# An encoder step whose input projection goes from plain column blocks, interleaved with the other work, to Strassen pairs done first

## The chip, the cores and the metric

The kernel runs on one core of a Trainium2 chip. The metric is the time of one execution in device microseconds (us). Names of the engines in the profile: PE is the matrix engine and PEld its weight loads, DVE the vector engine, ACT the scalar engine, POOL the GpSimd engine, SP the engine that issues the DMAs.

## The reference

One layer of a streaming encoder for 1088 tokens: 1024 of a new stream and 64 that continue another one. D is 1024, all in fp32.

```python
def hybrid_layer(x, p, st, past_k, past_v):
    h = rms_norm(x, p['norm_pre'])
    proj = h @ p['w_in']
    lru_x, lru_g, ssd_z, ssd_xbc, ssd_dt, cf_in, cf_g, sb_qkv, sb_g, merge = split_cols(proj, IN_SPLITS)
    lru_xc, lru_conv_new = causal_dwconv(lru_x, st['lru_conv'], p['lru_conv_w'], p['lru_conv_b'])    # 4 taps
    lru_h, lru_h_new = rg_lru(lru_xc, ...);  u_a = lru_h * jax.nn.silu(lru_g)
    xbc, ssd_conv_new = causal_dwconv(ssd_xbc, ...)                                                  # 4 taps
    y, ssd_new = ssd_scan(...);  u_b = rms_norm((y + D * xh) * jax.nn.silu(ssd_z), p['ssd_norm'])
    glu = cf_in[..., :CF_W] * jax.nn.sigmoid(cf_in[..., CF_W:])
    cfc, cf_conv_new = causal_dwconv(glu, ...)                                                       # 31 taps
    u_c = jax.nn.silu(layer_norm(cfc, ...)) * jax.nn.silu(cf_g)
    o = stick_breaking(q, k, v);  u_d = o * jax.nn.silu(sb_g)
    y_br = jnp.einsum('btnc,ncd->btnd', jnp.stack([u_a, u_b, u_c, u_d], axis=2), p['w_down'])
    mixed = jnp.sum(jax.nn.sigmoid(merge.reshape(bsz, t, N_BRANCH, D_MODEL)) * y_br, axis=2)
    return x + rms_norm(mixed @ p['w_out'], p['norm_post']), new
```

The input projection `h @ w_in` has 80 blocks of 128 columns and 8 columns more (`ssd_dt`). 32 of the 80 blocks are the gates of the four merges (`merge`).

## The kernel before

A product in fp32 is made of three matmuls on a high and a low part of each operand: `mm3` (L104 to L107) issues high by high, low by high and high by low. A column block of the projection takes 8 steps over D for each of three pieces of the tokens (256, 384 and 448 columns, `SPL`), so 72 matmuls. Its weights come by one DMA of 512 KB (`weights`, L90), ACT makes the high part (L97) and DVE the low one (L98).

The order of PE's instructions is written by hand: a generator (`Work`, `Feed`, L120 to L170) hands out one piece of a projection or of a merge at each `feed.step()`, and the chains of the other branches call it between their own steps. So the chains (on ACT, DVE and POOL) run while PE works on the projection. The other engines' orders come from the scheduler, by data dependences and by priorities (`ATT_PRIO`, `CONV_PRIO`, `W_PRIO`). Results of the projection go to the consumer from PSUM; a few (SiLU paths, `spill`) wait in DRAM. In order of time:

- the head (to 45 us): RMSNorm, transposes, the high and low part of h (`hh`, `hl`), beside the first two V blocks
- 45 to 580 us: the attention with 68 units (one of 8 heads by one of 8 query blocks of 128, and 4 units of the 64 tokens), fed with K, Q, V, gate, convolution-module and SiLU blocks. A unit is: score matmuls to PSUM `pz` (one buffer); two sigmoids on ACT (L430, L431); the causal mask on two 128x128 corners by POOL's affine_select (L435); a scan over the keys (L438) and a product (L439) on DVE; transposes on PE (L450), a copy on ACT (L452), the output matmuls (L468). The 31-tap convolution of the conv module runs on DVE at low priority (L239)
- 580 to 742 us: RG-LRU, with its projections, and the SSD's inputs (short convolutions, L239)
- 742 to 875 us: LayerNorm of the conv module, beside the first merge
- 875 to 1240 us: the SSD's scan in 9 chunks, beside merges 0 to 2. A merge takes a gate block (projection, sigmoid on ACT L689), the product with w_down (`down`, 12 matmuls for each piece), and DVE multiplies and adds (L698, L699)
- 1240 to 1336 us: the 8 gate blocks of the last merge, projections alone
- from 1336 us: the last merge's products with w_down, then w_out with the final RMSNorm

Of the kernel before, what the change touches and what calls it, by code (L numbers as in the profile page):

```python
# [16 lines left out]
D = 1024  # L17
EPS = 1e-6
SPL = ((0, 256), (256, 384), (640, 448))
NM = 448  # L20
# [4 lines left out]
OFF = 128 * 1088  # L25

LNA, LNB = (2, 2, 2), 5
ATT_PRIO, CONV_PRIO, W_PRIO, H_PRIO = 3000, 600, 300, 1000
# [17 lines left out]
def encoder_step(ctx, tc, x, prm, win, wdt, wdn, wout, lwa, lwx, ckT, cv_, ssd0, npre, npost, dtb, alog, dskip,  # L46
# [6 lines left out]
    hp = ctx.enter_context(tc.tile_pool(name="hT", bufs=1))  # L53
    wp = ctx.enter_context(tc.tile_pool(name="wts", bufs=2))
    ps = ctx.enter_context(tc.tile_pool(name="ps", bufs=1, space=PSUM))
    dr = ctx.enter_context(tc.tile_pool(name="scr", bufs=1, space=DRAM))
    uh_d = [dr.tile([128, 4, T], FT, name=f"uh{b}") for b in range(4)]
    ul_d = [dr.tile([128, 4, T], FT, name=f"ul{b}") for b in range(4)]
    xbc_d = dr.tile([128, 8, T], FT, name="xbc")
    sz_d = dr.tile([128, 4, T], FT, name="sz")  # L60
    lg_d = dr.tile([128, 4, T], FT, name="lg")
    cg_d = dr.tile([128, 4, T], FT, name="cg")
    cv_d = dr.tile([128, 4, T], FT, name="cv")

# [37 lines left out]
    hl = [hp.tile([128, 8, n], FR, name=f"hl{i}") for i, (_, n) in enumerate(SPL)]

# [4 lines left out]

    def rstd(st, r, n, w=1):
# [10 lines left out]
    class Work:  # L120
        """A chain of matrix work: its first stretch fetches operands, each later one is a piece of the tokens."""

        def __init__(self, gen):
            self.gen, self.ready, self.room = gen, False, False

        def prime(self):
            if not self.ready:
                self.ready = True
                next(self.gen)
            return self  # L130

        def step(self):
            self.prime()
            r = next(self.gen, self)
            self.room = r is True
            return r is not self

        def drain(self):
            while self.step():
                pass  # L140

    class Feed:
        """Matrix work issued between the steps of another chain."""

        def __init__(self):
            self.queue, self.later = [], []

        def add(self, *gens):
            self.queue.extend(Work(g) for g in gens)

        def defer(self, n, fn):
            self.later.append([n, fn])

        def step(self, n=1):
            for _ in range(n):
                while self.queue and not self.queue[0].step():
                    self.queue.pop(0)
                if len(self.queue) > 1 and self.queue[0].room:
                    self.queue[1].prime()
                for e in self.later:  # L160
                    e[0] -= 1
                for e in [e for e in self.later if e[0] <= 0]:
                    self.later.remove(e)
                    e[1]()

        def drain(self):
            while self.queue or self.later:
                self.step()

    feed = Feed()  # L170

    def project(p, n, i, hi, lo):
        for k in range(8):
            mm3(p[:, :n], hi[:, k, :], lo[:, k, :], hh[i][:, k, :], hl[i][:, k, :], k == 0, k == 7)

    def proj(chunk, evac, pt=pj, done=None):
        hi, lo = weights(win[chunk])
        yield
        for i, (t0, n) in enumerate(SPL):
            p = pt()  # L180
            project(p, n, i, hi, lo)
            evac(t0, n, p)
            if i == 2 and done is not None:
                done()
            yield True


    ctx.enter_context(tc.manual_schedule(engines={mybir.EngineType.PE}))
    warm = const.tile([128, 1], FT, name="warm")
    S.activation(warm, eps_t, AF.Sqrt)  # L190

    def head(hd, g_bc, tiles):
        w = len(tiles)
        st = hd.tile([128, 4 * w], FT, name="st", bufs=4)
        xs = []
        for e, i in enumerate(tiles):
            r = 128 if i < 8 else 64
            xt = hd.tile([128, D], FT, name="xt", bufs=9)
            dma(xt[:r], x[i * 128:i * 128 + r, :])
            if i == 0:  # L200
                dma(g_bc, ap(npre, 0, [[0, 128], [1, D]]))
            if r < 128:
                V.memset(st[r:, e:e + 1], 1.0)
            sq = hd.tile([128, D], FT, name="sq", bufs=1)
            S.activation(sq[:r], xt[:r], AF.Square, accum_out=st[:r, e:e + 1])
            xs.append(xt)
        rstd(st, 128, D, w)
        for e, i in enumerate(tiles):
            r = 128 if i < 8 else 64
            hn = hd.tile([128, D], FT, name="hn", bufs=4)  # L210
            V.scalar_tensor_tensor(hn[:r], xs[e][:r], st[:r, w + e:w + e + 1], g_bc[:r], op0=OP.mult, op1=OP.mult)
            j, o = WHERE[i]
            nk = 8 if i % 2 else 4
            for q in range(0, 8, nk):
                p = pz() if nk == 8 else pg()
                p3 = p.rearrange("p (k c) -> p k c", c=128)
                for k in range(nk):
                    PE.transpose(p3[:, k, :r], hn[:r, (q + k) * 128:(q + k + 1) * 128], ident[:r, :r])
                ks, dst = slice(q, q + nk), slice(o, o + r)
# [852 lines left out]
```

## Time and profile before

| | |
|---|---|
| time, median of 3 runs | 1494.03 us (1493.73 to 1494.9) |
| span of the profiled execution | 1490.9 us |
| median less that span | 3.1 us |
| PE busy | 1460.1 us (98%), 9157 matmuls |
| DVE busy | 921.1 us (62%) |
| ACT busy | 588.5 us (39%) |
| POOL busy | 118.9 us (8%) |
| MATMUL lines of the projection (L105 to L107 with `hh`, `hl`) | 637.6 + 631.8 + 631.5 us, 5760 matmuls |

The page gives the span of the profiled execution, without a time of its own; the 3.1 us between that span and the median of the runs stand in for what lies around it. A matmul's duration (some 330 ns) is its own length; since matmuls are pipelined, the next one starts earlier, and cost is read from the distance between starts. DVE and ACT instructions run one after another, so their durations add up, with a small overlap. The three projection lines above overlap in the same way and hold some 960 us of PE's time.

### The profile page before, as it was taken

The numbers are of one execution on the slowest core, as the hardware profiler recorded it, in microseconds if no ns is written. First come the engines' busy times: TensorE is split into PE (matmuls) and PEld (weight loads), VectorE is DVE, ScalarE is ACT, GpSimd is POOL, SyncE is SP. The second block draws the span as 40 slices with busy tenths as digits, with TensorE's granted clock in tenths as the row PEclk, the third lists the DMA queues.
The fourth block names the chain that finished last, engine by engine and source line by source line (L and its number), as shares of the span: only waits on it lengthen the run. The fifth ranks groups of instructions, "written<-read, shape, count | busy, mean of one in ns | idle before, by whom it ended". The sixth has DMA issues, their size and how long they took to land.

```text
span 1490.9 us, 23008 instructions
## 1 busy us (share of the span) xinstructions
PE 1460.1 (98%) x9157; PEld 1360.5 (91%) x9157; DVE 921.1 (62%) x1379; ACT 588.5 (39%) x1000; POOL 118.9 (8%) x157
## 2 busy tenths in 40 slices
PE   6999999999999999999999999999999999999997
PEld 5898999999999998999999999999999999999885
DVE  6289589579769955677765554656655541019433
ACT  6323434443453344666644322333332332124211
POOL 0003212231221222000000000000000000000000
PEclk9999999999999999999999999999999999999999
DMA  6232212313212323454433354222621234113322
GB/s 209 75 87 63 72 61 68 103 44 89 92 46 87 98 87 109 138 117 107 116 124 116 110 169 142 82 68 83 196 78 57 75 88 148 51 43 113 99 85 71
DMA packets 103339, 144.17 MB, mean 97 GB/s; under 512 B 20800, under 2 KB 82112, under 8 KB 103232
## 3 DMA queue, kind: packets, MB, share of 16 engines
q1 hardware_dynamic: 103232, 142.71, 31.9%
q8 instruction: 72, 1.18, 0.3%
q14 instruction: 35, 0.29, 0.1%
HBM read 97.95 MB, written 40.53 MB: 93 GB/s over the span
## 4 chain that ended last, share of the span: by engine, by line
PE 87%; issue 6%; DVE 4%; DMA 1%; ACT 1%; POOL 1%; SPq 0%; DVEq 0%; POOLq 0%; ACTq 0%
PE pj L105 24%; PE pj L106 24%; PE pj L107 24%; PE pg L468 2%; PE pg L450 2%; PE pg L106 1%; PE pg L107 1%; PE pg L105 1%; DVE cvo L239 1%; PE pz L417 1%; PE pz L418 1%; PE pg L878 1%; PE pg L736 1%; PE pg L871 1%; DMA g_bc<-in_npre_dram 0%
## 5 line engine op out<-in xcount | busy, mean ns | idle before, releaser
L105 PE MATMUL pj<-hh,w_hi 128*128 128x384 f32 (+2 forms) x1920 | 637.6, 332 | 1.7 <-ACT hh L220 1.7
L106 PE MATMUL pj<-hl,w_hi 128*128 128x384 f32 (+2 forms) x1920 | 631.8, 329 | 1.8 <-DVE hl L221 1.8
L107 PE MATMUL pj<-hh,w_lo 128*128 128x384 f32 (+2 forms) x1920 | 631.5, 329 | 0.0
L105 PEld LDWEIGHTS pj<-hh,w_hi 128*128 128x128 f32 x1920 | 363.6, 189 | 16.6 <-issue 2.1
L106 PEld LDWEIGHTS pj<-hl,w_hi 128*128 128x128 f32 x1920 | 363.7, 189 | 14.4 <-DVE hl L221 2.6
L107 PEld LDWEIGHTS pj<-hh,w_lo 128*128 128x128 f32 x1920 | 363.5, 189 | 11.0
L98 DVE TENSOR_TENSOR w_lo<-w_raw,w_hi 128x1024 fp32r<-128x1024 f32 x96 | 117.5, 1224 | 226.9 <-ACT w_hi L97 226.7
L97 ACT ACTIVATE w_hi<-w_raw 128x1024 fp32r<-128x1024 f32 x96 | 101.7, 1060 | 281.7 <-PE pj L106 262.6
L239 DVE SCALAR_TENSOR_TENSOR cvo<-cbuf,p_t,cvo 128x1118 f32<-128x1118 f32 x120 | 165.6, 1380 | 2.1
L105 PE MATMUL pj<-uh,w_hi 128*128 128x384 f32 (+2 forms) x384 | 126.2, 329 | 0.0
L107 PE MATMUL pj<-uh,w_lo 128*128 128x384 f32 (+2 forms) x384 | 126.2, 329 | 0.0
L106 PE MATMUL pj<-ul,w_hi 128*128 128x384 f32 (+2 forms) x384 | 126.1, 328 | 0.0
L438 DVE TENSOR_TENSOR_SCAN fb<-fb,ones 128x128 f32<-128x128 f32 (+8 forms) x68 | 90.0, 1324 | 38.0 <-POOL fb L435 37.4
L435 POOL TENSOR_SCALAR_AFFINE_SELECT beta<-beta 128x128 f32<-128x128 f32 (+1 forms) x72 | 78.2, 1086 | 14.4 <-ACT beta L431 13.7
L698 DVE TENSOR_TENSOR sg<-pj,sg 128x256 f32<-128x256 f32 (+2 forms) x48 | 25.7, 535 | 84.9 <-PE pj L107 80.6
L689 ACT ACTIVATE sg<-pj 128x256 f32<-128x256 f32 (+2 forms) x72 | 33.7, 468 | 112.2 <-PE pj L107 112.0
L105 PEld LDWEIGHTS pj<-uh,w_hi 128*128 128x128 f32 x384 | 72.7, 189 | 2.3
L106 PEld LDWEIGHTS pj<-ul,w_hi 128*128 128x128 f32 x384 | 72.6, 189 | 2.2
L107 PEld LDWEIGHTS pj<-uh,w_lo 128*128 128x128 f32 x384 | 72.6, 189 | 2.2
L435 POOL TENSOR_SCALAR_AFFINE_SELECT fb<-fb 128x128 f32<-128x128 f32 (+1 forms) x72 | 38.2, 530 | 449.2 <-ACT fb L430 354.4
L439 DVE TENSOR_TENSOR beta<-beta,fb 128x128 f32<-128x128 f32 (+8 forms) x68 | 50.3, 740 | 4.3 <-POOL beta L435 0.7
L452 ACT ACTIVATE wT<-pg 128x512 f32<-128x512 f32 (+3 forms) x96 | 43.3, 485 | 18.1 <-PE pg L450 17.8
(313 smaller groups left out, 1683.0 us busy)
## 6 DMA issues: line engine op xcount, KB each, us to landing
w_raw<-in_win_dram SPq DMA_DIRECT2D x80, 512.0 KB, 3.7
w_raw<-in_wdn_dram SPq DMA_DIRECT2D x16, 512.0 KB, 3.6
xt<-in_x_dram SPq DMA_DIRECT2D x8, 512.0 KB, 10.5
xbc<-xs SPq DMA_DIRECT2D x8, 512.0 KB, 2.6
xb<-xbc SPq DMA_DIRECT2D x8, 512.0 KB, 4.9
w_raw<-in_wout_dram SPq DMA_DIRECT2D x8, 512.0 KB, 3.7
xr<-in_x_dram SPq DMA_DIRECT2D x8, 512.0 KB, 3.8
out_y_dram<-yo SPq DMA_DIRECT2D x16, 256.0 KB, 2.3
```

Of the source, the lines that this page charges most:

```text
L97: S.activation(hi, r3, AF.Copy)
L98: V.tensor_sub(lo, r3, hi.bitcast(FT))
L105: PE.matmul(out, ah, bh, start=first, stop=False)
L106: PE.matmul(out, ah, bl, start=False, stop=False)
L107: PE.matmul(out, al, bh, start=False, stop=last)
L239: V.scalar_tensor_tensor(out[:, :n], b[:, i:i + n], w[:, i:i + 1], out[:, :n], op0=OP.mult, op1=OP.add)
L435: G.affine_select(t_[s, 1024 - w:1024], t_[s, 1024 - w:1024], pattern=[[-1, w]], compare_op=OP.is_gt, fill=fill, base=0, channel_multiplier=1)
L438: V.tensor_tensor_scan(F[:, rev], F[:, rev], ones[:, 0:1].to_broadcast([128, n]), 1.0, OP.mult, OP.mult)
L439: V.tensor_tensor(B[:, L:1024], B[:, L:1024], F[:, L + 1:1025], op=OP.mult)
L450: PE.transpose(p[:, (j - j0) * 128:(j - j0 + 1) * 128], B[:, L + j * 128:L + (j + 1) * 128], ident)
L452: S.activation(wT[:, j0:j1, :], p[:, :(j1 - j0) * 128].rearrange("p (j c) -> p j c", c=128), AF.Copy)
L689: S.activation(sg[:, :n], p[:, :n], AF.Sigmoid)
```

## The change

The 1088 tokens are cut into halves of 544 and each half into quarters of 272 columns. D is cut into two halves of 512. Two column blocks together are a 2 by 2 product of block matrices, and the Strassen-Winograd form does it with 7 products of 4 steps over D, not 8: per pair 7 x 2 x 12 = 168 matmuls of 272 columns. V's four blocks stay plain (`plain`), 38 pairs hold the other 76 blocks.

```diff
-SPL = ((0, 256), (256, 384), (640, 448))
+HT, QT = 544, 272
+SPL = ((0, 384), (384, 384), (768, 320))
+NSLOT, NR = 5, 4
+STEPS = (0, 1, 0, 1, 0, 1, 0, 1, 1, 0, 1, 0, 1, 0, 1, 0, 0)
...
+    V.tensor_sub(h12, h12, h11)
+    V.tensor_sub(h22, h22, h12)
+    quad_parts(6, h22)
+    V.tensor_sub(h11, h22, h11)
+    quad_parts(7, h11)
+    quad_parts(5, h12)
+    V.tensor_sub(h21, h21, h22)
...
+    ORDER = (1, 6, 2, 7, 5, 4, 3)
...
+            s1, s2, s4 = (wp.tile([128, 4, 128], FT, name=f"s{j}", bufs=1) for j in (1, 2, 4))
+            with tc.high_priority(offset=W_PRIO):
+                G.tensor_tensor(s1, a21, a22, op=OP.add)
+                G.tensor_tensor(s2, s1, a11, op=OP.subtract)
+                G.tensor_tensor(a21, a11, a21, op=OP.subtract)
+                G.tensor_tensor(s4, a12, s2, op=OP.subtract)
+            self.src = {1: a11, 6: s2, 2: a12, 7: a21, 5: s1, 4: a22, 3: s4}
...
+            for j in ORDER:
+                hi, lo = weights()
+                bh, bl = quad[j]
+                for q in range(2):
...
+                    for k in range(4):
+                        for z, (a_, b_) in enumerate(((hi, bh), (hi, bl), (lo, bh))):
+                            PE.matmul(p, a_[:, k], b_[:, k, s], start=new and k == 0 and z == 0, stop=k == 3 and z == 2,
...
+                        if j == 1:
+                            S.activation(r12, p, AF.Copy)
+                        elif j == 6:
+                            V.tensor_tensor(r12, p, r12, op=OP.add)
...
+    def silu_out(dst):
...
+            S.activation(t, r, AF.Sigmoid)
+            G.tensor_tensor(t, r, t, op=OP.mult)
+            dma(dst[:, i], t)
...
+    def gate_out(i, r):
+        S.activation(r, r, AF.Sigmoid)
+        dma(mg_d[:, i], r)
...
+                if bi == 0:
+                    V.tensor_tensor(m, p[:, :n], gi, op=OP.mult)
+                else:
+                    V.tensor_tensor(gi, p[:, :n], gi, op=OP.mult)
+                    G.tensor_tensor(m, m, gi, op=OP.add)
```

Each weight matrix of a product (7 per pair, 128x512) is split into its high and low part on ACT and DVE; four sums of weights are made on POOL. A product's PSUM bank is added up on DVE in 10 instructions of 272 columns per pair and 4 copies on ACT (`R`, four SBUF buffers), before the consumer sees the result. All consumers' results go to DRAM: q and k, SiLU paths, short-convolution outputs, the convolution module, and the 32 sigmoid gates.

The order of the stages changes as well: head, V, the dt projection with its softplus, then the 38 pairs one after another (q, k, the convolution module's input and the rest, the 16 pairs of gates last, with the LayerNorm in steps between their products), then the RG-LRU fed by steps of merge 0 (order 2, 0, 1, 3), the SSD's chunks fed by the rest of merge 0 and by merge 1, the attention fed by merge 2 (8 steps for each of 4 head pairs, `STEPS`), the last merge and w_out. A step of a merge holds the 12 matmuls of `down` alone, and its gate is loaded from DRAM.

DVE between the long convolution's taps, before. Names: `cvo` and `cbuf` are the convolution's output and input, `kl` a low part of k, `pj` a PSUM bank.

```order
L379 TENSOR_TENSOR kl1_537<-pj_4794,kh1_535 64x256
L239 SCALAR_TENSOR_TENSOR cvo_4549<-cbuf_4218,p_t_82,cvo_4549 128x1118 x2
L379 TENSOR_TENSOR kl0_536<-pj_4836,kh0_534 64x384
L239 SCALAR_TENSOR_TENSOR cvo_4549<-cbuf_4218,p_t_82,cvo_4549 128x1118
L379 TENSOR_TENSOR kl1_537<-pj_4836,kh1_535 64x384
```

DVE there after. L401 to L407 are the additions from a PSUM bank, L92 a low part of weights, L145 the taps of a long (1118) or a short (1092) convolution.

```order
L401 TENSOR_TENSOR r_4369<-bank_4421,r_4369 128x272
L92 TENSOR_TENSOR w_lo_4446<-w_raw_4173,w_hi_4445 128x512
L145 SCALAR_TENSOR_TENSOR u_4345<-u_4337,p_t_86,u_4345 128x1092
L445 MEMSET u_4353 128x1
L145 SCALAR_TENSOR_TENSOR u_3573<-u_3566,p_t_86,u_3573 128x1118
L92 TENSOR_TENSOR w_lo_4476<-s4_4178,w_hi_4475 128x512
L405 TENSOR_TENSOR r_4370<-bank_4479,r_4369 128x272
L143 TENSOR_SCALAR u_4361<-u_4353,p_t_86 128x1092
L405 TENSOR_TENSOR r_4370<-bank_4493,r_4369 128x272
L92 TENSOR_TENSOR w_lo_4508<-w_raw_4435,w_hi_4507 128x512
L145 SCALAR_TENSOR_TENSOR u_4361<-u_4353,p_t_86,u_4361 128x1092
L407 TENSOR_TENSOR r_4370<-bank_4511,r_4370 128x272
```

The taps now stand among the weight splits and the PSUM additions that the projection itself needs; pairs 4 to 20 hold all 124 taps of the long convolutions and 48 instructions of the short ones.

DVE in the attention at units of 896 keys, before. `fb` and `beta` are the two score tiles, `ud` the output times its gate.

```order
L438 SCALAR_TENSOR_TENSOR fb_528<-fb_528,ones 128x896
L439 TENSOR_TENSOR beta<-beta,fb_528 128x896
L297 TENSOR_TENSOR cbuf<-pj,sb 128x256
L438 SCALAR_TENSOR_TENSOR fb_529<-fb_529,ones 128x896
L439 TENSOR_TENSOR beta<-beta,fb_529 128x896
L297 TENSOR_TENSOR cbuf<-pj,sb 128x384
L481 TENSOR_TENSOR ud<-pg,g_t 128x128
L225 TENSOR_TENSOR udl<-ud,udh 128x128
```

The same units after.

```order
L949 SCALAR_TENSOR_TENSOR fb_12390<-fb_12390,ones 128x896
L950 TENSOR_TENSOR beta<-beta,fb_12390 128x896
L949 SCALAR_TENSOR_TENSOR fb_12391<-fb_12391,ones 128x896
L646 TENSOR_TENSOR gate<-pj_14291,gate 128x320
L950 TENSOR_TENSOR beta<-beta,fb_12391 128x896
L993 TENSOR_TENSOR ud<-pg_14306,g_t 128x128
L92 TENSOR_TENSOR w_lo_15172<-w_raw_15169,w_hi_15171 128x1024
L92 TENSOR_TENSOR udl<-ud,udh 128x128
```

Scan and product of each unit stay; of the work between them a multiplication of a merge and a weight split are left, once in about two units.

POOL in the projections, before (masks of the attention only) and after.

```order
L435 AFFINE_SELECT beta_1457<-beta_1457 128x128
L435 AFFINE_SELECT fb1_529<-fb1_529 128x128
L435 AFFINE_SELECT beta_1536<-beta_1536 128x128
L435 AFFINE_SELECT fb0_528<-fb0_528 128x128
L435 AFFINE_SELECT beta_1613<-beta_1613 128x128
```

```order
L372 TENSOR_TENSOR s1_2646<-w_raw_2643 128x512
L373 TENSOR_TENSOR s2_2647<-s1_2646,w_raw_2643 128x512
L374 TENSOR_TENSOR w_raw_2643<-w_raw_2643 128x512
L375 TENSOR_TENSOR s4_2648<-w_raw_2643,s2_2647 128x512
L419 TENSOR_TENSOR u_2807<-r_2577,u_2807 128x1088
L419 TENSOR_TENSOR u_2811<-r_2578,u_2811 128x1088
L372 TENSOR_TENSOR s1_2884<-w_raw_2881 128x512
```

POOL makes the weight sums of every pair and, for some pairs, the products of the SiLU paths; the masks come later, with the attention.

## Rows read from the trace of the kernel before

**Rows 1.** Page, span and busy time of each engine (share, instructions)

```profile
span 1490.9 us, 23008 instructions
PE 1460.1 (98%) x9157; PEld 1360.5 (91%) x9157; DVE 921.1 (62%) x1379; ACT 588.5 (39%) x1000; POOL 118.9 (8%) x157
```

**Rows 2.** Windows: stretch, its us, busy PE PEld DVE ACT POOL, PEclk, DMA, GB/s

```profile
0.00:45.00 45.00, 28.38 (x181) 25.68 (x182) 28.08 (x58) 27.52 (x51) 1.19 (x8) 0.96 0.56 189
45.00:580.00 535.00, 530.87 (x3600) 497.72 (x3599) 410.66 (x480) 222.89 (x455) 114.61 (x143) 1.00 0.25 76
...
875.00:1240.00 365.00, 363.43 (x2307) 342.22 (x2306) 201.28 (x379) 124.14 (x169) 1.46 (x3) 1.00 0.36 108
...
1336.00:1491.00 155.00, 147.17 (x712) 123.61 (x711) 80.67 (x189) 38.54 (x88) 0.00 (x0) 0.99 0.28 92
```

**Rows 3.** Timeline of PE, one gate block: start, us, instruction

```profile
1250.93 0.28 PE L105 MATMUL pj<-hh,w_hi 128*128 128x256 f32 x1
...
1253.80 0.34 PE L105 MATMUL pj<-hh,w_hi 128*128 128x384 f32 x1
...
1257.97 0.36 PE L105 MATMUL pj<-hh,w_hi 128*128 128x448 f32 x1
...
1262.92 0.28 PE L105 MATMUL pj<-hh,w_hi 128*128 128x256 f32 x1
```

**Rows 4.** Groups by form, DVE: busy, mean ns, idle before

```profile
L239 DVE SCALAR_TENSOR_TENSOR cvo<-cbuf,p_t,cvo 128x1118 f32<-128x1118 f32 x120 | 165.6, 1380 | 2.1
...
L698 DVE TENSOR_TENSOR sg<-pj,sg 128x256 f32<-128x256 f32 x16 | 6.8, 423 | 20.1 <-PE pj L107 20.0
...
L983 DVE TENSOR_TENSOR wp<-w_raw,wp 128x512 fp32r<-128x512 f32 x8 | 5.5, 682 | 0.7 <-ACT wp L982 0.7
```

**Rows 5.** Groups by form, POOL

```profile
L808 POOL MEMSET Sb<- 128x512 f32 x2 | 1.0, 526 | 295.0 <-DVE lng L225 295.0
...
masks.py:199 POOL TENSOR_SCALAR_AFFINE_SELECT ident<-ident 128x128 f32<-128x128 f32 x1 | 0.3, 292 | 0.1
```

**Rows 6.** Timeline of one attention unit, POOL beside DVE

```profile
311.12 2.02 DVE L438 TENSOR_TENSOR_SCAN fb<-fb,ones 128x896 f32<-128x896 f32 x1 [0.77 <-POOL fb L435]
...
311.60 1.62 POOL L435 TENSOR_SCALAR_AFFINE_SELECT beta<-beta 128x128 f32<-128x128 f32 x1 [0.52 <-ACT beta L431]
...
313.26 1.09 DVE L439 TENSOR_TENSOR beta<-beta,fb 128x896 f32<-128x896 f32 x1
```

**Rows 7.** Windows of the SSD: all, then L698, L699 and L98 alone (DVE)

```profile
908.00:1135.00 227.00, 225.55 (x1428) 212.34 (x1427) 130.92 (x245) 79.08 (x106) 0.00 (x0) 1.00 0.31 91
908.00:1135.00 227.00, 16.61 (x31) 1.00 0.31 91
908.00:1135.00 227.00, 16.60 (x31) 1.00 0.31 91
908.00:1135.00 227.00, 19.56 (x16) 1.00 0.31 91
```

**Rows 8.** Groups by form, ACT, in the RG-LRU

```profile
L617 ACT ACT_TABLE_LOAD x8 | 10.3, 1283 | 0.1
L617 ACT ACTIVATE gr<-pg,p_t 128x364 f32<-128x364 f32 x12 | 6.8, 565 | 0.4
L620 ACT ACTIVATE ga<-gr,lm 128x1092 f32<-128x1092 f32 x4 | 4.8, 1209 | 0.0
```

**Rows 9.** Page, groups: the attention's scan and product

```profile
L438 DVE TENSOR_TENSOR_SCAN fb<-fb,ones 128x128 f32<-128x128 f32 (+8 forms) x68 | 90.0, 1324 | 38.0 <-POOL fb L435 37.4
...
L439 DVE TENSOR_TENSOR beta<-beta,fb 128x128 f32<-128x128 f32 (+8 forms) x68 | 50.3, 740 | 4.3 <-POOL beta L435 0.7
```

**Rows 10.** DMA issues: KB each, us to landing

```profile
uh<-uh SPq DMA_DIRECT2D x4, 896.0 KB, 7.3
```

**Rows 11.** Waits of PE: total, times, longest

```profile
PE pg L218 <- DVE st L115: 10.0, 1, 10.0
PE pg L450 <- DVE beta L439: 2.4, 1, 2.4
```

**Rows 12.** Windows, 4 us behind that wait of 2.4 us

```profile
580.00:584.00 4.00, 4.00 (x40) 3.66 (x39) 0.89 (x3) 1.19 (x2) 1.60 (x4) 0.63 0.06 16
```

More of the change, by code (lines that the diff above doesn't have):

```diff
@@ L176, in proj @@
[L176 to L219, printed above, removed]
-                S.activation(hh[j][:, ks, dst], p3[:, :, :r], AF.Copy)
-                V.tensor_sub(hl[j][:, ks, dst], p3[:, :, :r], hh[j][:, ks, dst].bitcast(FT))
@@ new lines, in encoder_step @@
+    pd = pg()
+    for i in range(9):
+        r = 128 if i < 8 else 64
+        PE.transpose(pd[:r, i * 16:i * 16 + 16], dtr[:, i * 128:i * 128 + r], ident[:16, :16])
+    pd3 = pd[:, :144].rearrange("p (i c) -> p i c", c=16)
+    zb = dq.tile([128, 9, 8], FT, name="zb", bufs=1)
+    V.memset(zb, 0.0)
+    for r, i0, i1 in ((128, 0, 8), (64, 8, 9)):
+        V.tensor_tensor(zb[:r, i0:i1], pd3[:r, i0:i1, 0:8], dtb_t[:r, None, :].to_broadcast([r, i1 - i0, 8]), op=OP.add)
+        V.tensor_tensor(zb[:r, i0:i1], pd3[:r, i0:i1, 8:16], zb[:r, i0:i1], op=OP.add)
@@ new lines, in encoder_step, with ahead, next_weights, between @@
+    ready = []
+    todo = [(p, j) for p in range(len(pairs)) for j in ORDER]
+    def ahead(n):
+        while todo and len(ready) < n:
+            p, j = todo.pop(0)
+            pairs[p].prepare()
+            ready.append(split_w(pairs[p].src[j]))
+    def next_weights():
+        ahead(4)
+        return ready.pop(0)
+    for n, pair in enumerate(pairs):
+        if n == LN_FROM:
+            a3.close()
+            norm = layer_norm(a2.enter_context(tc.tile_pool(name="ln", bufs=1, side="right", reuse_waits="tile")))
+        count = [0]
+        def between(n=n, count=count):
+            count[0] += 1
+            ahead(3)
+            if count[0] == 2 and n + 1 < len(pairs):
+                pairs[n + 1].prepare()
+            if n >= LN_FROM and count[0] in (3, 7):
+                next(norm)
+        pair.run(next_weights, between)
@@ L925, in fourth @@
             dma(ul_d[1][:, :, t0:t0 + L], ul[:, :, :L].bitcast(FT))
+    feed.add(merge(1))
     prev = None
-    feed.step(LNB)
+    feed.step(2)
     for i in range(9):
@@ new lines, in encoder_step @@
+    feed.add(merge(2))
+    NU = 17
+    heads = {0: Head(0)}
+    heads[0].turn()
+    units = [Unit(c, i, h, c * NU + 2 * i + h) for c in range(4) for i in range(9) for h in ((0, 1) if i < 8 else (0,))]
+    units[0].scores()
+    for m, u in enumerate(units):
+        c, k = divmod(m, NU)
+        last = k == NU - 1
+        if not last:
+            units[m + 1].scores()
+        elif c < 3:
+            heads[c + 1] = Head(c + 1)
+            heads[c + 1].turn()
+        feed.step(STEPS[k])
+        if k and (units[m - 1].h == 1 or units[m - 1].i == 8):
+            units[m - 1].output(units[m - 2])
+        u.turn()
+        if last:
+            u.output(None)
+            if c < 3:
+                units[m + 1].scores()
```

1095 lines of the change are left out of this document (546 added, 549 removed).

## The prediction

> **What bounds the kernel now.** I read the page's first part, then the windows by stage, then single instructions. PE is busy 98% of the span, DVE 62%, ACT 39% [rows 1]. In the stage windows PE has 530.87 of 535 us in the attention and 363.43 of 365 in the SSD's stretch; only the head (28.38 of 45) and the end (147.17 of 155) leave it idle [rows 2]. The two longest waits of PE are 10.0 us at the head and 2.4 us [rows 11]. So the time is PE's work, and everything that DVE and ACT do is hidden by it. The question is therefore not only how much of PE's work goes, but whether something covers the chains of DVE and ACT where the work was taken away.
>
> **What a pair costs PE.** The distance between the starts of the three pieces of one block [rows 3] gives the pitch of a matmul, 24 per piece: 256 columns (1253.80 - 1250.93)/24 = 0.120 us, 384 columns 0.174, 448 columns 0.206; a whole block 1262.92 - 1250.93 = 11.99. Between 256 and 384 the pitch grows by 0.054 per 128 columns, so 272 columns take 0.120 + 0.007 = 0.126. A pair is 168 matmuls, 21.2 us, against 24.0 for its two blocks. On 38 pairs PE saves 2.8 x 38 = 106 us; V's four blocks, plain, take 4 x 96 x 0.126 = 48.5 against 47.9. If nothing else moved, the span would be some 1386.
>
> I now build the new span stage by stage, since the order is new: A head, V, dt; B pairs; C RG-LRU; D SSD; E attention; F last merge and w_out. Before, the pieces of the projection were spread over all the chains; now C, D and E have only the 96 pieces of four merges less the last, 12 matmuls each, to put beside them.
>
> **A, 88 us (82 to 98).** The first 45 us before have 45 - 28.38 = 16.6 idle [rows 2], which stay. To this come V 48.5, the transposes of the head (72 of 128 columns, about 0.12 each at the pitch above: 8), the dt products (64 matmuls of 272 columns: 8) and a stretch of softplus on DVE and ACT, some 20 short dependent instructions of 0.3 us (a 128-column one takes 292 ns on POOL [rows 5]; a 256-column DVE one 423 [rows 4]), which now stands alone ahead of the pairs: 7. The sum is 88.
>
> **B, 854 us (806 to 923).** PE's own part is 38 x 21.2 = 806. DVE decides whether it is reached. Per pair DVE splits 7 weight parts of 128x512 at 0.68 (L983, the same shape) and adds 10 PSUM pieces of 272 columns at 0.44 (423 ns at 256) [rows 4]: 4.8 + 4.4 = 9.2 us. That hides behind PE. But pairs 4 to 20 also carry all 124 long taps at 1.38 [rows 4], 171 us, and 48 short-convolution instructions, by the same speed per column 1.35, 65 us. So (171 + 65)/17 + 9.2 = 23.1 us of DVE per pair, and some 0.7 of memsets, state copies and the low part of q and k: 23.8, above PE's 21.2. A backlog of taps cannot wait long: the buffers of the convolutions are five. I take 17 x 23.8 = 405, 3 x 21.2 = 64 for the first three pairs, and 18 x 21.4 = 385 for the last 18, where DVE has room (the 0.2 is the LayerNorm's eight small products between them). Lower end: the taps run at the pitch of pipelined instructions and spread out, 806.
>
> The DMAs I cost at nothing: the results add some 45 MB of stores and loads (1088 columns of 128 x 4 bytes, 0.56 MB, for each of 80 blocks, one way or the other), 90 MB at most, but the 16 DMA engines are busy 0.25 of the attention's stretch and 0.36 of the SSD's [rows 2], and the load of a pair's weights is issued a pair ahead, 21 us. All of them go through SP's one queue, so a store that stands before that load and waits for a late convolution would hold it; the price is a pair's wait of a few us, a part of the upper end.
>
> POOL's four weight sums per pair are not in the trace before. Bounds: a 512-column memset at 0.526, and four times the 128-column affine_select, 4 x 0.292 = 1.17 [rows 5]. I take the upper, nearer since a sum reads two tiles: 4.7 us per pair, under 21.2, so POOL itself does not bound. But in the attention POOL's 128-column select beside a DVE scan took 1.62 us in place of 0.29, and ended at 313.22, just behind the scan's end at 313.14 [rows 6]. The two engines exclude one another there. If all 4.7 us of sums fall on taps and splits, which read two tiles of SBUF, 17 x 4.7 = 80 are added, of which I put 69 into the upper end, 923, since the PSUM additions leave POOL some room.
>
> The Trainium skill says in "SBUF — State Buffer", section "Who interferes with whom", that a DVE instruction with two SBUF inputs and a GpSimd instruction that reads SBUF exclude one another, and the loser is blocked for the whole instruction. The trace agrees, with the 1.62 us. The Trainium skill's "GPSIMD Engine Reference", section "3.1 Elementwise — side-by-side cycle accounting", has 4497 ns for a sum of 2048 columns, so 1.12 us at 512 as an estimate; by that price 17 pairs would gain 76 us where I have up to 80, and no run shown here has the instruction.
>
> **C, RG-LRU, 68 us (55 to 85).** Its chain was hidden. ACT has per channel block six sigmoids of 364 columns at 0.565, exp, tanh and root at 1.2 each, three table loads at 1.28 [rows 8], two high parts of 1092 columns (1.1 each, by the same speed per column) and a weight split for the merge (1.1): 3.4 + 3.6 + 3.8 + 2.2 + 1.1 = 14.1. Four of them are 56, and 12 to load the operands and to fill the chain. Merge 0 gives only 12 steps here.
>
> **D, SSD, 150 us (125 to 175).** In the stretch from 908 to 1135 us, 6.9 chunks, DVE is busy 130.92 us, of which 16.61 and 16.60 are the merge's additions and 19.56 weight splits [rows 7]: 78.1 remain, 11.3 per chunk. With the merge's one multiplication per step (1.5 per chunk) and 2 to 3 us in which a chunk waits for its own PE and ACT steps, a chunk takes 15 to 16. 8.5 chunks (the last has 64 tokens) are 132 and some 14 go into the first operands, the small sums and the tail, so 146, rounded to 150 for the fewer steps behind which its waits can lie.
>
> **E, attention, 248 us (215 to 300).** The scan and the product hold DVE for 90.0 + 50.3 = 140.3 us on 68 units [rows 9]. POOL's mask can't run beside them [rows 6], so each unit adds a gap of about 0.3 (0.292 alone [rows 5]): 22. The output's multiplication and low part, the merge's product and its weight split add some 0.7 per unit: 48. This is 210, DVE alone, at full packing. Small units (128 and 256 keys) have too little DVE work to cover the way score, sigmoid, mask, scan, product, transpose, copy, output: 26 more; loading of the first head pair from DRAM and four changes of head pair: 12. Before, the projection covered all of it (530.87 of 535 [rows 2]). PE's own work there is some 163, my estimate from the scores, transposes and outputs at the pitch of rows 3.
>
> **F, 160 us (153 to 165).** Before it is 155 from 1336 us on [rows 2]. The operands of the last merge are now those that the attention has just written, and the largest of their loads lands in 7.3 us [rows 10]; about 5 of it are exposed.
>
> **Sum.** 88 + 854 + 68 + 150 + 248 + 160 = 1568, and the 3.1 us by which the median of the runs stands above the span: **1571 us**, 5% slower than 1494.03. In other words: PE saves 106, and C to E and DVE's taps give back some 185, since the filler was spent in B.
>
> **Rivals.** All three go by the same stages.
>
> - *The chains pack* (faster). DVE and ACT of consecutive units and chunks run back to back, the taps spread, and PE's saving remains. Then B 806, A 84, F 155, C 55, D 125, E 215: 1440 and 3, **1443**. The point from which it decides: A + B + F at the least are 82 + 806 + 153 = 1041, so C + D + E must stay under 1491 - 1041 = 450, and under 400 if B comes out as I say. For it: DVE and ACT are in the trace idle 38% and 61%, and the attention's E at 215 is only DVE's packing. Against: PSUM's `pz` has one buffer, so a unit's scores wait for the sigmoids before.
> - *The exclusion of POOL and DVE with PE's clock* (slower still). B 923, and in C to E PE often stands. Behind the wait of 2.4 us the granted clock is 0.63 in a 4-us window [rows 12], which is full clock (2.4 GHz) for a part and the lower level (1.2 GHz) for the rest. With the chains of E waiting for PE's transposes at that level, E 285, C 75, D 170: 88 + 923 + 75 + 170 + 285 + 160 = 1701, and since not all of it comes together, **1680**.
> - *A pair is no cheaper than its two blocks*. Weight splits, seven per pair and each for 24 matmuls alone, come too late in the light pairs as well, and the pairs take 24 us as before: B 912, the rest as forecast, 1626 and 3, **1629**.
>
> **Chances.** The forecast has 0.60: what I know of the DVE's work in B, D and E comes from measured rows, and all six stages would have to end low at once to gain. The packing has 0.19, the exclusion with the clock 0.15, the dear pair 0.06. Faster by over 0.2% is the packing, 0.19. Within 0.2%, about what a measurement of this kernel can tell from none, is the edge between packing and forecast, 0.02. Slower has 0.79. The forecast's own range is 1500 to 1640. Over the cases it goes from 1445 to 1680: half of the packing lies below it and a third of the exclusion above.
>
> **What would show it.** In the profile after: a pair's 168 matmuls in 21 to 22 us behind pair 20 and 23 to 25 between pairs 4 and 20, with PE waiting there for a low part of weights or a bank of PSUM that DVE has not read; sums on POOL of about 1.1 us, longer beside taps; PE busy about 65% in the attention with DVE at 85% or more, and idle ahead of transposes for L950. Wrong would be: pairs at 21.2 throughout (then A and B alone gain 50 us), or an attention under 210 us, which would need scans that are shorter than in the rows, or a SSD chunk under 13 us.

## The result and the profile after

The changed kernel takes 1759.18 us (4 runs, 1758.23 to 1760.57), the kernel before 1493.88 (4 runs). The ratio is 1.1774, 95% interval 1.1757 to 1.179: 265 us slower, where 77 were forecast. The time lies outside the range of 1445 to 1680. All six stages came out above their terms. Each stage is measured from its first matmul to the first of the next:

| stage | forecast | measured |
|---|---|---|
| A head, V, dt | 88 | 103.1 |
| B 38 pairs | 854 (806 to 923) | 916.3 |
| C RG-LRU, to the SSD's first product | 68 | 106.9 |
| D SSD | 150 | 176.3 |
| E attention | 248 | 291.3 |
| F last merge, w_out | 160 | 164.3 |

The page of the changed kernel, first lines. Against [rows 1], PE's busy time is the same though it has 106 us less to do; a lower granted clock in places (0.914 on the mean of the span, 0.997 before) is a part of that. DVE has 287 us more and POOL 347 more.

```profile
span 1758.2 us, 26712 instructions
PE 1462.8 (83%) x10185; PEld 1374.9 (78%) x10185; DVE 1207.6 (69%) x1807; ACT 666.6 (38%) x1156; POOL 465.9 (26%) x385
```

Its windows: the heavy pairs 4 to 20, the LayerNorm's pairs 26 to 29 with one before, the light pairs 30 to 38, then C, D, E and F (columns as in rows 2).

```profile
168.50:606.60 438.10, 386.49 (x2858) 380.35 (x2857) 436.83 (x501) 139.00 (x241) 178.26 (x86) 0.94 0.25 86
697.50:828.90 131.40, 115.03 (x855) 113.31 (x854) 86.51 (x131) 58.30 (x85) 30.60 (x20) 0.94 0.39 134
828.90:1019.30 190.40, 190.40 (x1514) 190.03 (x1512) 93.12 (x159) 72.89 (x119) 46.55 (x34) 1.00 0.27 98
1019.40:1126.30 106.90, 51.45 (x241) 48.38 (x241) 53.74 (x78) 61.75 (x68) 11.51 (x7) 0.72 0.56 191
1126.30:1302.60 176.30, 132.91 (x780) 116.84 (x780) 138.39 (x281) 50.02 (x72) 21.62 (x19) 0.84 0.50 145
1302.60:1593.90 291.30, 209.61 (x1513) 175.72 (x1513) 179.91 (x246) 137.66 (x295) 114.37 (x174) 0.87 0.47 132
1593.90:1758.20 164.30, 150.79 (x722) 128.96 (x720) 79.70 (x175) 37.89 (x89) 0.00 (x0) 0.96 0.36 113
```

DVE is full in the heavy pairs (436.83 of 438.10), PE in the light ones (190.40 of 190.40). In C, D and E no engine is full: PE has 48%, 75% and 72%, DVE 50%, 78% and 62%, ACT 58%, 28% and 47%. Before, PE was full beside the same chains [rows 2]. The granted clock falls to 0.72 to 0.87 of 2.4 GHz in the stretches in which PE waits, so a part of each runs at 1.2 GHz.

The first matmul of pair 31 and of pair 32 in PE's timeline: 21.09 us, as forecast (21.2).

```profile
850.45 0.29 PE L393 MATMUL bank<-Bh,w_hi 128*128 128x272 f32 x1
...
871.54 0.29 PE L393 MATMUL bank<-Bh,w_hi 128*128 128x272 f32 x1
```

DVE's groups by form: against [rows 4], a long tap takes 1676 ns, not 1380, and a weight split 777 to 901, not 682.

```profile
L145 DVE SCALAR_TENSOR_TENSOR u<-u,p_t 128x1118 f32<-128x1118 f32 x120 | 201.1, 1676 | 0.2
L92 DVE TENSOR_TENSOR w_lo<-w_raw,w_hi 128x512 fp32r<-128x512 f32 x160 | 144.0, 901 | 18.8 <-ACT w_hi L91 13.8
...
L92 DVE TENSOR_TENSOR w_lo<-s,w_hi 128x512 fp32r<-128x512 f32 x114 | 88.5, 777 | 73.2 <-ACT w_hi L91 71.2
```

Why, in the timeline of one sum on POOL and the tap beside it:

```profile
380.93 1.29 POOL L372 TENSOR_TENSOR s<-w_raw 128x512 f32<-128x512 f32 x1 [0.63 <-DVE w_lo L92]
381.12 2.28 DVE L145 SCALAR_TENSOR_TENSOR u<-u,p_t 128x1118 f32<-128x1118 f32 x1
```

The tap starts 0.19 us behind the sum, ends 1.18 us behind the sum's end, and takes 2.28 us in place of 1.38: for most of the sum it made no headway. In [rows 6] it was POOL that stood still. The Trainium skill says in "SBUF — State Buffer", section "Who interferes with whom", that issue order, and not the shape of the operation, decides who blocks. Both traces agree: the sum here and the scan there began first, and it is the other instruction that took longer (2.28 here, 1.62 there).

PE's waits (total, times, longest). New against [rows 11] are the PSUM additions in the heavy pairs (`r`); the SSD's folding (`yt`: DVE adds up halves of a chunk's output ahead of PE's last product of the chunk); one wait at the start of E (`vT`, the V of the first head pair) and three each for `kh` and `kl`, the high and low part of K, at the changes of head pair; one at the end of C (`lt`, DVE's input to the SSD's first product); and two at the start of C (`xg`, the high part of the RG-LRU's input, and `w_hi`, weights of the merge). `lns` is the LayerNorm.

```profile
PE bank L393 <- DVE r L405: 43.8, 21, 5.3
PE pg L835 <- DVE yt L833: 39.4, 9, 5.9
PE pg L905 <- DMA vT<-vs: 22.9, 1, 22.9
...
PE pz L758 <- DVE lt L755: 16.7, 1, 16.7
PE pg L522 <- DVE lns L510: 16.4, 3, 5.8
PE pg L86 <- ACT xg L91: 14.2, 1, 14.2
PE pz L928 <- DMA kh<-khs: 12.3, 3, 5.5
PE pj L86 <- ACT w_hi L91: 10.5, 1, 10.5
...
PE pz L929 <- DMA kl<-kls: 5.9, 3, 2.0
```

What stands ahead of `lt` on DVE, and of vT's load in SP's queue:

```profile
1124.30 1.29 DVE L92 TENSOR_TENSOR ual<-gx,uah 128x1088 fp32r<-128x1088 f32 x1 [3.88 <-ACT uah L91]
1125.51 0.68 DVE L755 TENSOR_TENSOR lt<-tri_le,adh 128x512 fp32r<-128x512 f32 x1
```

```profile
1305.57 0.59 SPq L845 DMA_DIRECT2D ul<-uol  x1
1306.22 0.64 SPq L873 DMA_DIRECT2D cv<-in_cv_dram  x1
...
1318.60 0.32 SPq L896 DMA_DIRECT2D vT<-vs  x1
```

`lt` follows on the last split of the RG-LRU (`ual`), so its wait of 16.7 us is the tail of C's last channel block, and it counts in C's 106.9. The loads of the first head pair stand behind the SSD's last store (`ul`), SP issues 16 of them one after the other in 12 us ahead of vT, and vT is what PE needs first.

### The profile page after: what moved, and what is told of

Same layout as the page of the kernel before. It is cut to its first block, busy times and chain, and to the rows that moved or that the text cites. A ratio compares the mean times of both kernels' runs of the same rounds, so it can differ in the third digit from the quotient of the medians.

```text
span 1758.2 us, 26712 instructions
## 1 busy us (share of the span) xinstructions
PE 1462.8 (83%) x10185; PEld 1374.9 (78%) x10185; DVE 1207.6 (69%) x1807; ACT 666.6 (38%) x1156; POOL 465.9 (26%) x385
## 4 chain that ended last, share of the span: by engine, by line
PE 41%; DVE 16%; issue 13%; DMA 4%; POOL 4%; ACT 4%; SPq 1%; POOLq 0%; DVEq 0%; ACTq 0%
PE bank L393 24%; DVE u L145 6%; PE pj L86 3%; PE pj L87 3%; PE pj L88 3%; DVE w_lo L92 2%; POOL beta L946 1%; POOL fb L946 1%; PE pg L86 1%; PE pg L88 1%; PE pg L87 1%; DMA lnx<-cv 1%; POOL m L647 1%; DMA w_raw<-in_wdn_dram 1%; DVE fb L949 1%
## 5 line engine op out<-in xcount | busy, mean ns | idle before, releaser
L393 PE MATMUL bank<-Bh,w_hi 128*128 128x272 f32 x1216 | 366.1, 301 | 51.6 <-DVE r L405 43.8
L393 PE MATMUL bank<-Bh,w_lo 128*128 128x272 f32 x1216 | 361.8, 298 | 3.3 <-DVE w_lo L92 3.3
L393 PE MATMUL bank<-Bl,w_hi 128*128 128x272 f32 x1216 | 361.6, 297 | 0.0
L393 PEld LDWEIGHTS bank<-Bh,w_hi 128*128 128x128 f32 x1216 | 240.8, 198 | 58.1 <-issue 42.1
L393 PE MATMUL bank<-Th,w_lo 128*128 128x272 f32 x912 | 265.4, 291 | 0.0
L393 PE MATMUL bank<-Th,w_hi 128*128 128x272 f32 x912 | 265.3, 291 | 0.0
L393 PE MATMUL bank<-Tl,w_hi 128*128 128x272 f32 x912 | 263.5, 289 | 0.0
L145 DVE SCALAR_TENSOR_TENSOR u<-u,p_t 128x1118 f32<-128x1118 f32 (+1 forms) x156 | 258.8, 1660 | 0.2
L393 PEld LDWEIGHTS bank<-Bh,w_lo 128*128 128x128 f32 x1216 | 240.6, 198 | 3.6 <-DVE w_lo L92 3.6
L393 PEld LDWEIGHTS bank<-Bl,w_hi 128*128 128x128 f32 x1216 | 240.9, 198 | 0.2
L92 DVE TENSOR_TENSOR w_lo<-w_raw,w_hi 128x512 fp32r<-128x512 f32 (+1 forms) x176 | 166.7, 948 | 29.2 <-ACT w_hi L91 24.0
L86 PE MATMUL pj<-uh,w_hi 128*128 128x384 f32 (+1 forms) x384 | 142.3, 371 | 14.2 <-ACT w_hi L91 10.5
L949 DVE TENSOR_TENSOR_SCAN fb<-fb,ones 128x128 f32<-128x128 f32 (+8 forms) x68 | 91.6, 1348 | 82.5 <-POOL fb L946 82.3
L92 DVE TENSOR_TENSOR w_lo<-s,w_hi 128x512 fp32r<-128x512 f32 x114 | 88.5, 777 | 73.2 <-ACT w_hi L91 71.2
```

The source lines that it names most:

```text
L86: PE.matmul(out, ah, bh, start=first, stop=False)
L92: V.tensor_sub(lo, src, hi.bitcast(FT))
L145: V.scalar_tensor_tensor(out[:, :n], b[:, i:i + n], w[:, i:i + 1], out[:, :n], op0=OP.mult, op1=OP.add)
L393: PE.matmul(p, a_[:, k], b_[:, k, s], start=new and k == 0 and z == 0, stop=k == 3 and z == 2, skip_group_check=True)
L949: V.tensor_tensor_scan(F[:, rev], F[:, rev], ones[:, 0:1].to_broadcast([128, n]), 1.0, OP.mult, OP.mult)
```

## The experiments

Single runs unless said; the kernel before took 1492.45 to 1493.22 us beside them. "The pairs" are from the first matmul of the first pair to the end of the last. Stages that an edit doesn't touch differ by some us from run to run (A from 99.9 to 104.4), so a stage's length says more than a few us of the whole time.

**The weight sums left out.**

```diff
-                G.tensor_tensor(s1, a21, a22, op=OP.add)
-                G.tensor_tensor(s2, s1, a11, op=OP.subtract)
-                G.tensor_tensor(a21, a11, a21, op=OP.subtract)
-                G.tensor_tensor(s4, a12, s2, op=OP.subtract)
-            self.src = {1: a11, 6: s2, 2: a12, 7: a21, 5: s1, 4: a22, 3: s4}
+            self.src = {1: a11, 6: a21, 2: a12, 7: a21, 5: a22, 4: a22, 3: a12}
```

> Changed kernel with POOL's four weight sums per pair left out (the seven products take plain quarters of the weights instead, so the projection's values are not the reference's; all else, DMAs and splits too, stays). Theory 1, exclusion of DVE and POOL: in pairs 4 to 20 the long taps took 1.69 us and the weight splits 0.84 to 1.04, against 1.38 and 0.68 in the kernel before, some 76 us in all; most of it is the sums' doing. So taps fall to 1.4 to 1.5 us, heavy pairs from 25.8 to about 22, the 38 pairs from 919 to about 860, the time to about 1700. Theory 2, DVE simply has too many instructions there: heavy pairs stay at 25 or more, the time moves by less than 15 us.

1695.15 us; the pairs 853.4, 63 less. Pairs 4 to 20 take 22.3 on the mean. Twelve of the 17 take 21.1 to 21.4; five with a SiLU product on POOL nearby still take 22.6 to 26.7. The taps take 1.49 us. The second line is the window of pairs 4 to 20:

```profile
L145 DVE SCALAR_TENSOR_TENSOR u<-u,p_t 128x1118 f32<-128x1118 f32 x120 | 178.3, 1486 | 0.2
```

```profile
166.90:546.50 379.60, 367.29 (x2859) 365.37 (x2857) 378.63 (x501) 140.65 (x241) 46.06 (x18) 0.98 0.28 100
```

So theory 1 is right: the same number of DVE instructions (501) keep it busy for 378.63 us, where it was 436.83 with POOL's sums beside them. DVE is busy all the time here too. In the pairs without work on POOL its own work comes up to 21.1 us, but not above.

**The sums on DVE.** `G.` becomes `V.` in the four lines.

> Changed kernel with the four weight sums of each pair on DVE in place of POOL. Theory 1, exclusion: DVE gains 4 x 0.68 us of work per pair but its taps and splits run at 1.4 and 0.7 again, so the heavy pairs stay near 25 us and the time within 1730 to 1765. Theory 2, DVE's own work bounds and the exclusion costs little: 17 x 2.7 = 46 us more, about 1805.

1744.15 us, pairs 903.2; pairs 4 to 20 take 24.7 on the mean. DVE does 152 instructions more, and the kernel is 15 us faster for it. Theory 1 holds.

**The pairs spread.**

```diff
+    pairs = [cf(0), q_(0), k_(0), q_(2), k_(2), lx(0), cf(1), dg(0), gates(0), dg(2), gates(1), lx(2), sx(0),
+             cf(2), cg(0), gates(2), cg(2), gates(3), sx(2), cf(3), lg(0), lg(2), sz(0), sz(2), sx(4), sx(6)]
+    LN_FROM = len(pairs)
+    pairs += [gates(i) for i in range(4, 16)]
-            if n >= LN_FROM and count[0] in (3, 7):
+            if n >= LN_FROM and count[0] == 3:
```

> Changed kernel with another order of the pairs: each of the four convolution-module pairs is followed by four pairs with light work on DVE, four gate pairs among them, and the LayerNorm takes one step per pair (twelve pairs) in place of two. Theory 1, the backlog of taps in 17 pairs and the LayerNorm's closely set steps cost the 110 us by which the pairs lie above 38 x 21.1: DVE's 590 us fit into 26 pairs of 21.1, the pairs fall from 919 to 820 to 845, the time to about 1670. Theory 2, the exclusion moves with the taps and every pair that has taps waits: the pairs stay above 880.

1708.07 us, pairs 864.2: between the two theories. The LayerNorm's twelve pairs take 21.1 to 21.7 each, so its closely set steps were the loss there. Most pairs with long taps still take 22 to 29.

**The kernel before without its filler in the attention.**

```diff
                 feed.add(*extra)
+            feed.drain()
             fed = 0
```

> Kernel before, with the projections that were fed into the attention's units run ahead of each group of 17 units and nothing fed between the units. No Strassen, same work. Theory 1, what was lost is the cover: 68 bare units at about 4 us, 270 us, of which 165 is PE's own work, so about 105 us more than before, 1580 to 1620. Theory 2, units without filler pack (my forecast's rival): under 1530.

1603.56 us, 111 more with the same 9157 matmuls: theory 1. (A few pieces of K and Q at each change of head pair are not handed out by `feed`, and stay where they were.) PE now waits for the units (2.4 before, in [rows 11]), and is busy 45 us longer than in [rows 1]:

```profile
span 1601.8 us, 22985 instructions
...
PE 1505.0 (94%) x9157; PEld 1382.0 (86%) x9157; DVE 920.3 (57%) x1379; ACT 592.7 (37%) x1000; POOL 92.9 (6%) x157
...
PE pg L450 <- DVE beta L439: 57.4, 45, 2.6
```

So taking the projection out from between the units costs more than Strassen saves on all 38 pairs (106). The units don't pack. The granted clock is 0.967 here and 0.997 in the kernel before; how much of the 45 us is the clock isn't separated.

**Three scores in flight.** PSUM split 2, 2 and 2 x 2 banks, three `fb` and `beta`:

```diff
-            units[m + 1].scores()
+            units[m + 2].scores()
```

> Changed kernel with the attention's scores issued two units ahead in place of one (two score banks pairs in PSUM, two instead of three of the other kinds, a third fb and beta buffer). Theory 1, with one unit ahead the scores wait on PE behind the transposes of the unit before, and these for DVE's product, so sigmoid, mask and scan of the next unit start late (DVE idle 82 us ahead of the scans): the attention falls from 293 to 225 to 250 us, the time to 1715 to 1735. Theory 2, DVE and POOL exclude each other and bound the unit: stays within 5 us of 1759.

1754.88 us; first score to last output 261.7, before the edit 266.6. Theory 1's range is missed. PE's wait for the sigmoids ahead of the scores goes (16.9 us before, 1.5 now), and that for `kh` and `kl` is halved (18.2, now 9.5), since the edit also issues the next head pair's loads a unit earlier. But the wait for PSUM banks that the output's multiplication (ud) frees grows from 10.1 us to 32.1:

```profile
PE pg L974 <- DVE ud L1006: 32.1, 13, 6.0
```

The edit itself leaves two of these banks in place of three, so what earlier scores alone would give isn't shown. The number fits theory 2, but that the exclusion bounds the unit isn't shown either.

**Filler that does nothing.**

```diff
+        p = pj()
+        for z in range(4):
+            PE.matmul(p[:, :384], tri_gt, heads[c].kh[0][:, :384], start=z == 0, stop=z == 3)
         u.turn()
```

> Changed kernel with four matmuls of 384 columns added ahead of each unit's transposes in the attention, into a PSUM bank that nothing reads (272 matmuls, 47 us of PE at full clock). Theory 1, PE's clock (0.87 in the attention) lengthens the chain: the filler keeps it near 1.00 and the attention stays or falls by up to 15 us. Theory 2, PE's order is the bound: it grows by 30 to 50 us.

1768.81 us. The units take 279.0, 12 more, for 47 us of added matmuls: neither theory. The units of the changed kernel and of this one:

```profile
1327.30:1593.90 266.60, 207.76 (x1506) 173.91 (x1504) 178.06 (x240) 136.34 (x292) 114.00 (x173) 0.89 0.44 125
```

```profile
1326.00:1605.00 279.00, 244.41 (x1778) 217.21 (x1776) 179.39 (x240) 138.52 (x292) 119.78 (x173) 0.93 0.42 120
```

The clock rises from 0.89 to 0.93 and the time doesn't fall. So raising the clock in this way doesn't pay; some three quarters of the filler found idle time. The price of the lower clock alone isn't separated, since the filler also stands in PE's order ahead of the transposes.

**The SSD's last step later.** `prev.fourth()` moves behind `ch.second()`; `yt` and `yz` get two buffers.

> Changed kernel with the SSD's last step of a chunk (its PE product waits for DVE's folding, 39.4 us in 9 waits) issued behind the next chunk's second step, and two buffers for its two tiles. Theory 1, the wait is latency that other work covers: the SSD's stretch falls from 181 to 150 to 160 us, the time to 1730 to 1740. Theory 2, DVE with 140 us of work and its in-order queue bounds: falls by less than 10 us.

1748.52 us; D 163.2, 13 less: between the two theories. The wait for the folding is halved, and DVE is now at 87%:

```profile
1125.60:1289.00 163.40, 125.41 (x780) 108.36 (x780) 141.75 (x281) 49.38 (x73) 19.93 (x19) 0.91 0.54 158
```

```profile
PE pg L835 <- DVE yt L833: 19.5, 9, 3.5
```

**The first heads' operands early.** The pool `at` and `Head(0)` move ahead of the SSD.

> Changed kernel with the attention's first operands loaded ahead of the SSD in place of behind it (their tiles are taken before the SSD's). Theory 1, PE's wait of 22.9 us for vT goes: 1735 to 1742. Theory 2, the loads are late for another reason (SP's queue, or the SSD's own loads are held up): within 8 us of 1759.

1749.23 us, in neither range. The wait for vT goes, and one for the SSD's own operands (`xb`, `Ct`) of the same length appears: D is 193.1 in place of 176.3, E 267.6 in place of 291.3. This is theory 2's reason. In SP's one queue the SSD's loads now stand behind those of the head pair:

```profile
PE pg L805 <- DMA Ct<-xbc: 22.4, 1, 22.4
```

```profile
1122.07 0.46 SPq L727 DMA_DIRECT2D cv<-in_cv_dram  x1
...
1136.85 0.32 SPq L747 DMA_DIRECT2D vT<-vs  x1
1137.99 0.56 SPq L782 DMA_DIRECT2D xb<-xbc  x1
```

They were not issued early, but directly behind the last store of the RG-LRU. Loads among the steps of C or D, or vT ahead of the others, were not tried.

**The split of the output deferred**, on top of three scores: `split(uh, ul, ud)` and its stores go into a list that is worked off two units later.

> The kernel with three scores in flight, and the split of a unit pair's output (a copy on ACT that stood in ACT's order ahead of the next unit's sigmoids; ACT idle 43 us for ud in front of it) issued two units later. Theory 1, ACT's order holds the attention: it falls from 262 (scores to last output) to 220 to 240, the time from 1755 to 1715 to 1735. Theory 2, the chain through PE at its lower clock holds it, whatever the order: within 8 us of 1755.

1744.01 us; the units take 253.4. This is 11 us less than with three scores alone, half of the least that theory 1 said; PE still waits 32.3 us for ud. Neither theory's range is met. The attention stays a chain through the queues of four engines, in which the next link has so far taken the place of a removed one.

**Spread pairs, one tap per product.** The taps go into a list; each product of a pair issues one.

> The kernel with spread pairs, and one tap of a long convolution issued per product of a pair (7 per pair) in place of all at once at low priority. Theory 1, the pairs with taps still took 23 to 29 us because DVE's order packed more taps into a pair than it can run beside POOL: no pair with long taps above 24 us, the pairs fall from 865 to 825 to 845, the time from 1708 to 1670 to 1690. Theory 2, the exclusion alone holds them: above 1700.

1712.94 us, pairs 863.9: no gain. But the edit didn't do what it was meant to do. DVE's order is the scheduler's, and in the trace the pairs hold the same number of long taps as in the run before: 9, 8, 8 and 6 behind the first module pair in both, and up to 11 elsewhere, not 7. So this run tests neither theory. One of the pairs, with eleven taps and a SiLU product on POOL (POOL 15.15 us, DVE full):

```profile
590.30:619.70 29.40, 23.98 (x170) 23.57 (x169) 29.33 (x30) 7.68 (x13) 15.15 (x6) 0.88 0.20 74
```

**The same without POOL's sums and SiLU products.**

> The kernel with spread and paced pairs, with POOL's weight sums left out (plain quarters of the weights in their place) and POOL's products of the SiLU paths left out (the sigmoid alone is stored); values differ from the reference's. Theory 1, POOL beside DVE's two-input instructions is what still holds the pairs at 864: taps at 1.40 us, no pair above 22.5 but the first and those with the module's own product on POOL, the pairs 815 to 825, the time 1655 to 1675. Theory 2, order and count of DVE's instructions hold them: the pairs stay above 845.

1652.58 us. The pairs take 806.4, which is 38 x 21.2, and PE is busy all of it: a little below theory 1's ranges. The first takes 22.2, no other more than 21.7, and the taps are back at [rows 4]:

```profile
L477 DVE SCALAR_TENSOR_TENSOR u<-u,p_t 128x1118 f32<-128x1118 f32 x120 | 165.2, 1376 | 0.6
```

```profile
104.13:910.55 806.42, 806.42 (x6402) 805.55 (x6401) 593.17 (x921) 329.63 (x537) 13.84 (x10) 1.00 0.32 115
```

So the 110 us that B lay above PE's own time have two parts: the order of the pairs with the LayerNorm's steps (52, by the run with spread pairs) and POOL's work beside DVE (57, by this run against the one before). And with B at its floor the kernel is still 160 us behind.

**The edits that keep the computation, together**: spread and paced pairs, the SSD's last step later, early heads, three scores, the deferred split.

> All edits that gained together: spread pairs with paced taps, SSD's last step later, first head's operands loaded early, three scores in flight, split deferred. If the stages are independent the gains add up: pairs 80, SSD 13, early loads 10, attention 5 to 40: 1600 to 1650. The kernel before stays faster: 1.07 to 1.10. If the gains hide one another: above 1660.

1682.97 us (4 runs, 1677.95 to 1684.94), ratio to the kernel before 1.1263 (1.124 to 1.1287). This is above 1660: the gains hide one another. Pairs 864.2, D 184.8, units 254.9: the early loads take back in D what the later step gave. No version here beats the kernel before.

## Why the prediction was wrong

The side was right and the size wrong: 77 us were forecast, 265 came. Of the 190 us by which the span lies above the sum of 1568, B has 62, E 43, C 39, D 26, A 15 and F 4. In B the price of DVE's work beside POOL failed; in C, D and E the waits at the changes of stage and of head pair failed, and in D the work and the waits of a chunk too. Step by step:

- *A pair costs PE 21.2 us*: right, 21.09 in the light pairs and 806.4 for all 38 in the kernel without POOL's work.
- *17 heavy pairs at 23.8, POOL's exclusion only in the upper end*: this step failed, twice. DVE's own instructions were added up at full length and came to more than PE's 21.2; without POOL they fit into 21.1. They overlap more than I took: in pairs 4 to 20 without the sums the 501 instructions last some 417 us one by one, and DVE is busy 378.63, so 38 us or 2.2 per pair less. The exclusion, which I had read in [rows 6] and left out of the sum, lifts the pairs to (606.6 - 168.5)/17 = 25.8. I forecast 23.8 as own work; it was 21.1 at most, and some 4.7 of waiting for POOL (3.4 for the sums, the rest in pairs with SiLU products). A sum took 1.29 us at best, above my upper bound of 1.17. By the Trainium skill's "GPSIMD Engine Reference", section "3.1 Elementwise — side-by-side cycle accounting", 1.12 was the estimate; the measurement decides.
- *18 light pairs at 21.4*: wrong for pair 21, which took 27.3, and for the LayerNorm's. Pairs 26, 27 and 29 took 28 to 30, with two of its steps each; one step per pair cured it. That a load, a fold and a PE product stood too close there is my reading of PE's three waits for `lns`. Why pair 21 is long isn't settled.
- *C 68, with 12 for the start*: the start alone has two waits of 24.7 us in all (xg and w_hi), and the end has the 16.7 for `lt`. The channel blocks themselves follow each other at some 16.3 us (three periods between the first and the last start of the product L699, 1067.6 and 1116.4), near my 14.1. I took every change of stage for short: those to C, D and E hold 14.2 + 10.5 + 16.7 + 22.9 = 64 us of PE waiting, for which I had 12 + 14 + 12 = 38, with other things in them. At the change to E the loads stand in SP's queue behind the last store of the stage before; at the change to D DVE first ends the RG-LRU's last block. Moving the loads of one (E) only moved the wait. For C it wasn't tried.
- *D, 11.3 us of DVE per chunk*: I divided 78.1 us [rows 7] by 6.9 chunks from an assumed period. The trace of before has six in that window, as the count of one of the chunk's instructions shows, so 13.0. And PE's wait for the folding alone is 39.4 us, where I had taken 2 to 3 us of all waits per chunk, some 21. Of the 39.4, 13 us could be had back.

```profile
L847 DVE TENSOR_TENSOR cbm<-pg,tri_le 128x512 f32<-128x512 f32 x6 | 4.1, 689 | 0.3 <-PE pg L845 0.3
```

- *E 248, of which 210 are DVE alone*: the forecast had DVE at 85% or more; in the units it is at 67% (178.06 of 266.6), some 10 us less than the 188 of work that I had in the 210. The term that failed most is the 12 us for loading the first head pair and for the changes of pair. DVE stands 24.8 us ahead of the first scan, while PE waits for vT, and 17.8 ahead of the first scan of the other three head pairs, while PE waits for their `kh` and `kl` (12.3 and 5.9). The other 64 scans have 39.9 of the 82.5 us before them, 0.6 each where I took 0.3:

```profile
L949 DVE TENSOR_TENSOR_SCAN fb<-fb,ones 128x128 f32<-128x128 f32 (+8 forms) x68 | 91.6, 1348 | 82.5 <-POOL fb L946 82.3
```

```profile
1330.20 0.49 DVE L949 TENSOR_TENSOR_SCAN fb<-fb,ones 128x128 f32<-128x128 f32 x1 [24.81 <-POOL fb L946]
...
1401.41 0.48 DVE L949 TENSOR_TENSOR_SCAN fb<-fb,ones 128x128 f32<-128x128 f32 x1 [7.38 <-POOL fb L946]
```

What closes the loop is not settled to a single link: neither the scores' place (with a PSUM bank less), nor ACT's order, nor the filler that raised PE's clock gave more than 11 us.
- *DMAs at nothing*: the engines had room (a share of 0.56 in C, 0.25 in the heavy pairs), but the one queue did not: the head pair's loads, moved ahead, made those of D late.
- *F 160*: 164.3. *A 88*: 103.1, with 30.0 us of PE idle where 24 were taken and 73.1 us of PE busy where 64 were, a part of it at a lower clock (0.94 in A).

Of the rivals, the packing is refuted by C, D and E themselves, and by the unfed kernel before (1603.56). That a pair is no cheaper is refuted. The exclusion is shown. The rival that joins it with PE's clock came nearest, with a chance of 0.15: B 923, D 170 and E 285 against 916, 176 and 291 measured; only its C (75 against 107) and the A that it shared with the forecast were far off. This is in part luck, since its reason for D and E, the clock, was not shown: the clock was lower there (0.84 and 0.87), but no run separates its price from the waits.

Where the 106 us went: A, B and F without POOL's work in B are 104 + 806 + 164 = 1074. To draw level with the span before, 1491, that leaves 417 for C, D and E, whose waits PE's projection had filled before. They took 574.5. The nearly 160 us between are what these stages cost without the filler, their changes included; the rest of the loss is B's, which lies 916.3 - 806.4 = 110 above that floor.

## What to carry to other kernels

Matrix work that fills the waits of other chains can be worth more than its own time (111 us here, for work that was only moved): before saving it or moving it ahead, find out what the chains cost bare, by a run with the same work unfed. When work goes to POOL to spare DVE, count the DVE instructions that run beside it; here the kernel was faster with the sums on DVE itself. A chunk's or unit's cost is found by dividing by the count of an instruction in the window, not by an assumed period. And after an edit to the order, look in the trace whether the order has changed.

## What the runs showed of the hardware

Either engine can lose: POOL's 128-column select waited for DVE's scan (1.62 us for 0.29), DVE's tap for POOL's sum (2.28 for 1.38). DVE instructions with one SBUF input lose too: the 12 copies of three columns (L441) took 530 ns on the mean in the changed kernel, 353 without the sums and 162 without the SiLU products as well; those of [rows 4]'s kernel took 161. A POOL sum of 128x512 takes 1.29 us at the least, and a product of 128x1088 takes 2.51. SP issued the 16 loads ahead of vT's in 12 us, one after the other. In C, where PE waits for half of the time, the granted clock is 0.72; in the light pairs, where it never waits, 1.00.
